# The heads stage of a GLA layer: DMA queues in the source's order, gates and states asked later, reciprocal roots on VectorE

## The chip, the cores and the metric

The kernel runs on one core of one Trainium2 chip. A core has five engines that work side by side, each with its own queue of instructions: TensorE (PE, matmul; PEld is its weight load), VectorE (DVE), ScalarE (ACT), GpSimd (POOL) and SyncE (SP, which here only issues DMAs). The metric is the time of one execution in device microseconds.

## The reference

One step of a two-layer streaming encoder, width D = 2048: 512 rows of a prompt, and 8 running streams of 16 rows each, 640 rows in all. Layer 0 is stick-breaking attention, layer 1 gated linear attention (GLA) with 4 heads, keys of 256 and values of 512. The change lies in layer 1. Cut to what matters:

```python
def gla_chunk(S, inp):                     # per chunk, S is the state (DK, DV) of a head
    q, k, v, g = inp                       # g = log a_t, the decay of each key dimension
    b = jnp.cumsum(g, axis=1); b_last = b[:, -1]
    q_in = q * jnp.exp(b)
    a = tril(einsum('bchd,bshd->bhcs', q_in, k * jnp.exp(-b)))
    o = einsum('bhcs,bshe->bche', a, v) + einsum('bchd,bhde->bche', q_in, S)
    S = exp(b_last)[..., None] * S + einsum('bshd,bshe->bhde', k * exp(b_last[:, None] - b), v)
    return S, o

q, k, v, r, a_lr = split(h @ w_in, ...)    # the plain products of layer 1
g = log_sigmoid(a_lr @ w_a2 + b_a) / 16
o = o * rsqrt(mean(o * o, axis=-1) + EPS) * g_out      # one norm per row and head
y = (o * silu(r)) @ w_out
```

## The kernel before, in words

Products in fp32 are done as three matmuls of a type that keeps fewer bits: `split` and `halves` make of each weight piece a high part on ScalarE (`wh`, L134, a cast) and the rest on VectorE (`wl`, L135, a subtraction). A raw piece `wr` is 128 x 1024 of float32, 0.52 MB, in two buffers that SP loads (L71).

The change concerns the heads stage of layer 1, L1508 to 1971. When it begins, the values `gv`, the gates `gr` and head 0's `gq` and `gk` are on their way to scratch tensors in DRAM. In the stage TensorE runs the rest of the layer's input product (`others`, `plain`, L632): the `q` and `k` columns of heads 1 to 3 in 24 weight pieces, 48 matmuls each on the two halves of the 640 rows (L654), two pieces to a result. A result leaves TensorE's bank by a ScalarE copy `pl` (L1519), and ScalarE stores it (L1521). The product has two banks. In the end stands the first part of the output product (`share`, L700) with its copies `y` (L708) and sums (L705).

Between the pieces of this product, side lanes put in their own work, each a Python generator:

- `decays`: loads `wa2`, `q`, `k` of a head, makes the decay (matmul L1647, Abs, Exp, Ln, scan, Exp: L1648 to 1673).
- `prompt_lane`: 16 units (4 heads x 4 chunks of 128 rows). `fetch` loads two tiles `v`, `fetch_gate` one tile `gate` (L71). A unit makes scores, output `o` and state `S`; `normed` (L1580) squares and sums on ScalarE (L1584) and asks `rstd_of` for the reciprocal root: mean plus EPS on VectorE (`on_ms`, L232), then a power of -0.5 on GpSimd (`on_r`, L234). `scaled_by` (L1588, ScalarE) applies it; `leave` (L1602) turns it, multiplies the gate in (L1607), and ScalarE stores it as `og` (L1610).
- `sample_lane`: the 8 streams, all at once for each head; their old states `s0` are loaded by GpSimd's DMAs (`move`, L78), eight buffers, and stored updated. `vst`, a stack of their values, is loaded by GpSimd too. One norm per head.
- `fetches`: loads `og` back and splits it for the output product.

`step(t)` in a lane and `side.after(t, f)` count in `pe["now"]`, a sum of estimated TensorE times that runs as the code is written out; they decide where in the written order a piece of work stands. TensorE's queue is the written order throughout. The queues of the other engines are put in order by a scheduler, which may move an instruction ahead of others of its engine. Both kernels give each DMA of SP and ScalarE the next of eight completion semaphores in turn; a DMA waits until the one that used its semaphore before has landed.

## Time and profile before

| what | value |
|---|---|
| median of 3 runs | 2514.42 us (2511.73 to 2514.44) |
| profiled execution | 2514.76 us, span 2513.0 us |
| granted clock of TensorE, mean | 0.984 |
| TensorE busy | 2427.7 us, 97% |
| VectorE, ScalarE, GpSimd busy | 63%, 40%, 5% |
| TensorE, share of the chain that ended last | 78% |

The profile is of one execution. The prediction shows rows of these views: busy time by windows; waits (engine, line and tile, released by which instruction: total, times, longest); timelines (start, duration, engine, line, operation, out<-in, shape, and in brackets the idle time before it with its releaser). Times in rows are us from the start of the span. The heads stage runs from about 1960 to 2400 us.

### The profile page before, as it was taken

The numbers are of one execution on the slowest core, as the hardware profiler recorded it, in microseconds if no ns is written. First come the engines' busy times: TensorE is split into PE (matmuls) and PEld (weight loads), VectorE is DVE, ScalarE is ACT, GpSimd is POOL, SyncE is SP. The second block draws the span as 40 slices with busy tenths as digits, with TensorE's granted clock in tenths as the row PEclk, the third lists the DMA queues.
The fourth block names the chain that finished last, engine by engine and source line by source line (L and its number), as shares of the span: only waits on it lengthen the run. The fifth ranks groups of instructions, "written<-read, shape, count | busy, mean of one in ns | idle before, by whom it ended". The sixth has DMA issues, their size and how long they took to land.

```text
span 2513.0 us, 43986 instructions
## 1 busy us (share of the span) xinstructions
PE 2427.7 (97%) x17561; PEld 2150.1 (86%) x17561; DVE 1580.6 (63%) x2566; ACT 994.1 (40%) x1731; POOL 135.2 (5%) x350
## 2 busy tenths in 40 slices
PE   6899999999999999999999999999999999999998
PEld 4589999899999998888887767999999989987776
DVE  5575555555666655666776568766676466675556
ACT  4332222222223334555544245333333455565223
POOL 0010000000000000000000000000000212332000
PEclk8899999999999999999999999999999999999999
DMA  9966666667664357777874664443534758976634
GB/s 343 330 210 216 224 205 208 221 214 226 209 202 126 110 166 227 256 243 236 259 235 146 187 226 134 129 118 110 145 104 117 209 183 271 294 265 218 226 114 147
DMA packets 487502, 503.12 MB, mean 200 GB/s; under 512 B 42746, under 2 KB 387202, under 8 KB 487170
## 3 DMA queue, kind: packets, MB, share of 16 engines
q1 hardware_dynamic: 456978, 441.85, 55.8%
q0 software_dynamic: 12848, 41.43, 4.8%
q10 hardware_dynamic: 17472, 17.04, 2.0%
q8 instruction: 138, 2.26, 0.4%
q14 instruction: 66, 0.54, 0.1%
HBM read 411.10 MB, written 89.13 MB: 199 GB/s over the span
## 4 chain that ended last, share of the span: by engine, by line
PE 78%; DMA 6%; DVE 4%; ACT 3%; issue 1%; SPq 0%; POOL 0%; ACTq 0%; POOLq 0%; DVEq 0%
PE ps_mm L595 40%; PE ps_mm L700 9%; PE ps_mm L654 9%; PE ps_mm L369 3%; PE ps_tp L1086 2%; DMA gv<-kr 2%; PE ps_tp L1559 2%; PE ps_mm L519 1%; PE ps_tp L1046 1%; PE ps_tp L1138 1%; PE ps_z L1022 1%; PE ps_z L180 1%; PE ps_mm L2042 1%; PE ps_z L1100 1%; PE ps_z L222 1%
## 5 line engine op out<-in xcount | busy, mean ns | idle before, releaser
L595 PE MATMUL ps_mm<-sums,wh 128*128 128x320 f32 x2752 | 613.5, 311 | 1.5 <-ACT wh L134 1.5
L595 PE MATMUL ps_mm<-h,wh 128*128 128x320 f32 x2064 | 462.8, 312 | 4.7 <-DVE u L601 4.7
L595 PEld LDWEIGHTS ps_mm<-sums,wh 128*128 128x128 f32 x2752 | 457.9, 188 | 10.4 <-issue 7.4
L595 PE MATMUL ps_mm<-sums,wl 128*128 128x320 f32 x1376 | 425.3, 309 | 0.7 <-DVE wl L135 0.7
L135 DVE TENSOR_TENSOR wl<-wr,wh 128x1024 fp32r<-128x1024 f32 x193 | 236.1, 1224 | 232.3 <-ACT wh L134 228.9
L595 PEld LDWEIGHTS ps_mm<-h,wh 128*128 128x128 f32 x2064 | 344.0, 188 | 20.7 <-issue 14.6
L134 ACT CAST wh<-wb 128x1024 fp32r<-128x1024 f32 x170 | 178.4, 1050 | 426.5 <-PE ps_mm L595 350.3
L134 ACT CAST wh<-wr 128x1024 fp32r<-128x1024 f32 x193 | 202.5, 1050 | 329.3 <-PE ps_mm L595 186.7
L595 PE MATMUL ps_mm<-h,wl 128*128 128x320 f32 x1032 | 319.3, 309 | 0.0
L654 PE MATMUL ps_mm<-h,wh 128*128 128x320 f32 x1152 | 265.7, 318 | 8.8 <-ACT pl L1519 6.3
L595 PEld LDWEIGHTS ps_mm<-sums,wl 128*128 128x128 f32 x1376 | 258.3, 188 | 1.0 <-DVE wl L135 1.0
L135 DVE TENSOR_TENSOR wl<-wb,wh 128x1024 fp32r<-128x1024 f32 x170 | 207.8, 1223 | 62.7 <-ACT wh L134 62.5
L654 PEld LDWEIGHTS ps_mm<-h,wh 128*128 128x128 f32 x1152 | 193.7, 190 | 23.5 <-issue 8.9
L700 PE MATMUL ps_mm<-wh,ogh 128*128 128x512 f32 x450 | 197.3, 438 | 7.2 <-ACT y L708 4.0
L595 PEld LDWEIGHTS ps_mm<-h,wl 128*128 128x128 f32 x1032 | 194.2, 188 | 0.0
L654 PE MATMUL ps_mm<-h,wl 128*128 128x320 f32 x576 | 178.8, 310 | 0.0
L700 PE MATMUL ps_mm<-wl,ogh 128*128 128x512 f32 x450 | 177.2, 394 | 0.3 <-DVE wl L135 0.3
L700 PE MATMUL ps_mm<-wh,ogl 128*128 128x512 f32 x450 | 177.2, 394 | 0.3 <-DVE ogl L135 0.3
L700 PEld LDWEIGHTS ps_mm<-wh,ogh 128*128 128x128 f32 x450 | 85.0, 189 | 35.7 <-issue 14.3
L654 PEld LDWEIGHTS ps_mm<-h,wl 128*128 128x128 f32 x576 | 109.1, 189 | 0.2 <-DVE wl L135 0.2
L700 PEld LDWEIGHTS ps_mm<-wh,ogl 128*128 128x128 f32 x450 | 84.7, 188 | 20.3 <-DVE ogl L135 0.7
L519 PE MATMUL ps_mm<-wh,h 128*128 128x512 f32 x252 | 93.2, 431 | 5.7 <-ACT h L134 3.7
(359 smaller groups left out, 3712.9 us busy)
## 6 DMA issues: line engine op xcount, KB each, us to landing
ar<-in_w_ada_dram SPq DMA_DIRECT2D x160, 512.0 KB
wb<-in_sb_w_in_dram SPq DMA_DIRECT2D x82, 512.0 KB
kc<-in_cache_sb_k_dram SPq DMA_DIRECT2D x64, 512.0 KB
vc<-in_cache_sb_v_dram SPq DMA_DIRECT2D x64, 512.0 KB
wr<-in_gla_w_in_dram SPq DMA_DIRECT2D x51, 512.0 KB
wb<-in_gla_w_in_dram SPq DMA_DIRECT2D x45, 512.0 KB
wr<-in_sb_w_in_dram SPq DMA_DIRECT2D x44, 512.0 KB
ar<-in_w_ada_dram SPq DMA_DIRECT2D x64, 256.0 KB
```

The source lines that it names most:

```text
L134: nc.scalar.copy(hi, x)
L135: (e or dve).tensor_tensor(lo, x, hi.bitcast(F32), op=ALU.subtract)
L180: mm(acc[32 * q:32 * q + 32, :w], cT[:, kt + m, :], by(cT[:, kt + m, :], rs[m // each][:, m % each, q, :]), start=kt + m == 0, stop=kt + m ...
L222: mm(acc[32 * j:32 * j + 32, :256], cT[:, kt + m, :], by(cT[:, kt + m, :], r[:, 256 * j:256 * j + 256]), start=kt + m == 0, stop=kt + m == ...
L369: mm(acc[a], l[:, c], by(l[:, c], r[:, k2, :]), start=kt == k0 and first, stop=kt == k0 + nk - 1 and last)
L519: mm(acc[a], l, by(l, r[:, e, :]), start=j == 0 and e == 0 and begun, stop=j == 7 and e == 1 and last)
L595: mm(acc, l[:, k, :], by(l[:, k, :], r), start=start and k == 0 and first, stop=k == 7 and last, skip_group_check=True)
L654: mm(acc[nt], l[:, k, :], by(l[:, k, :], r), start=k0 == 8 and k == 0 and first, stop=k0 == 0 and k == 7 and last)
L700: mm(acc, l, by(l, r[:, e, :]), start=i == 0 and e == 0 and first, stop=i == 1 and e == 1 and last)
L1022: mm(z[:, :n], q[:, hh, qs], by(q[:, hh, qs], k[:, hh, :n]), start=True, stop=True)
L1086: turn_block(tp[:, P * c:P * c + P], block(kc[:, c, P * hh:P * hh + P]), ident)
L1559: mm(out, l[a], by(l[a], r[b]), start=start and n == 0, stop=stop and n == 2, skip_group_check=True)
```

## The change

Three things, all in layer 1's heads stage.

1. For this stage SP's and GpSimd's queues too are in the written order, as TensorE's is. The scheduler still orders ScalarE's and VectorE's.
2. Places in the written order: the first two gates are asked at 40 and 44 us of estimated TensorE time instead of 14 and 16 (each later one 6 instead of 7 us after the store that frees its buffer), the eight first states from 26 on instead of from 18, the sample lane's first fetch at 30 instead of 12.
3. The 20 norms' reciprocal roots come from nine VectorE operations on 128 x 1 (`rstd_dve`: the mean, a first guess from the float's bits, one cubic and one quadratic refinement) instead of one on VectorE and one on GpSimd. Other norms of the kernel still use `rstd_of`.

```diff
+I32 = mybir.dt.int32
...
+    def rstd_dve(pool, ss, n, name):
+
+        ms, r, t, u = (pool.tile([P, 1], F32, tag=f"{name}_{x}", name=f"{name}_{x}", bufs=2 if x == "r" else 1) for x in ("ms", "r", "t", "u"))
+        dve.tensor_scalar(ms, ss, 1.0 / n, EPS, op0=ALU.mult, op1=ALU.add)
+        dve.tensor_scalar(r.bitcast(I32), ms.bitcast(I32), -0.5, float(0x5F3759DF), op0=ALU.mult, op1=ALU.add)
+        for cubic in (True, False):
+            dve.scalar_tensor_tensor(t, r, ms, r, op0=ALU.mult, op1=ALU.mult)
+            if cubic:
+                dve.tensor_scalar(u, t, 0.375, -1.25, op0=ALU.mult, op1=ALU.add)
+                dve.tensor_scalar(u, t, u, 1.875, op0=ALU.mult, op1=ALU.add)
+            else:
+                dve.tensor_scalar(u, t, -0.5, 1.5, op0=ALU.mult, op1=ALU.add)
+            dve.tensor_tensor(r, r, u, op=ALU.mult)
+        return r
...
             tc.tile_pool(name="w4", bufs=1, reuse_waits="tile") as w4:
+        loads = ExitStack()
+        loads.enter_context(tc.manual_schedule(engines={mybir.EngineType.SP, mybir.EngineType.Pool}))
...
-            return on, rstd_of(gl, s1, 512, "on"), o
+            return on, rstd_dve(gl, s1, 512, "on"), o
...
-                side.after(14.0 + 2.0 * u, lambda u=u: fetch_gate(u))
+                side.after(40.0 + 4.0 * u, lambda u=u: fetch_gate(u))
...
-                    side.after(7.0, lambda: fetch_gate(u + GP))
+                    side.after(6.0, lambda: fetch_gate(u + GP))
...
-            side.after(18.0 + 2.0 * n, ask)
+            side.after(26.0 + 2.0 * n, ask)
...
-            yield step(12.0)
+            yield step(30.0)
             here = fetch(0)
...
         side.finish()
+        loads.close()
```

The change adds lines, so that L1519 of before is L1537 after, L1588 is L1606, L708 is L724, L71 is L72. In the rows below, numbers behind names count tiles: `wr` is a raw weight piece, `gr_3` a store of layer 1's gate, `alr_in` the low-rank input of the decay.

SP's queue at the start of the stage, before (weight pieces 2 and 3 of the plain product are `wr_20615` and `wr_20677`):

```order
L71 DMA wr_20615<-in_gla_w_in_dram 128x8x128
L71 DMA wr_20677<-in_gla_w_in_dram 128x8x128
L74 DMA gr_3_106<-out_20288 128x640
L74 DMA gr_3_106<-out_20289 128x640
L71 DMA alr_in_20577<-alr_d_115 96x640
L71 DMA wa2_20593<-wa2_d_116 96x256
L71 DMA v_20595<-gv_0_0_107 128x512
L71 DMA v_20596<-gv_0_1_108 128x512
L71 DMA q_20665<-gq_0_95 128x1280
L71 DMA k_20666<-gk_0_99 128x1280
L71 DMA v_20693<-gv_0_0_107 128x512
L71 DMA v_20694<-gv_0_1_108 128x512
```

Then follow two more `v`, three gates, and weight pieces 4 and 5. SP's queue at the same place after (pieces 2 to 5 are `wr_20617`, `wr_20679`, `wr_20757`, `wr_20835`):

```order
L72 DMA alr_in_20579<-alr_d_115 96x640
L72 DMA wa2_20595<-wa2_d_116 96x256
L72 DMA v_20597<-gv_0_0_107 128x512
L72 DMA v_20598<-gv_0_1_108 128x512
L72 DMA wr_20617<-in_gla_w_in_dram 128x8x128
L72 DMA q_20667<-gq_0_95 128x1280
L72 DMA k_20668<-gk_0_99 128x1280
L72 DMA wr_20679<-in_gla_w_in_dram 128x8x128
L72 DMA v_20695<-gv_0_0_107 128x512
L72 DMA v_20696<-gv_0_1_108 128x512
L72 DMA wr_20757<-in_gla_w_in_dram 128x8x128
L72 DMA wr_20835<-in_gla_w_in_dram 128x8x128
```

The weight pieces 2 and 3 went from ahead of `gr` to behind the first `v` and behind `k`; pieces 4 and 5 went ahead of the gates, which now follow two more `v`.

ScalarE's queue at the store of the first `gq`, before:

```order
L1519 COPY pl_20679<-ps_mm_20553 128x320
L1648 ACTIVATE b_20697<-ps_tp_20715,cols_81 128x320
L1521 DMA gq_1_96<-pl_20679 128x640
L1651 ACT_TABLE_LOAD
L1651 ACTIVATE b_20697<-b_20697 128x640
L1652 ACT_TABLE_LOAD
```

And after:

```order
L1537 COPY pl_20681<-ps_mm_20555 128x320
L1666 ACTIVATE b_20699<-ps_tp_20717,cols_81 128x320
L1539 DMA gq_1_96<-pl_20681 128x640
L1669 ACT_TABLE_LOAD
L1669 ACTIVATE b_20699<-b_20699 128x640
L135 CAST wh_20753<-wr_20679 128x1024
L1670 ACT_TABLE_LOAD
```

The cast of weight piece 3, which stood ahead of this store, now stands in the middle of the decay's chain. In both the copy `pl` of the next result comes some ten rows further down.

GpSimd's queue, in words: before, eight states stood ahead of the six `vst` loads; after, three states, the six `vst` loads, five states. In between the 20 powers are gone.

ScalarE's queue at the last prompt unit, near a copy `y` of the output product, before:

```order
L1584 ACTIVATE on_24232,oss_24231<-ps_tp_24179 128x512
L1857 CAST kst0_20581<-ps_tp_24202 48x512
L1610 DMA og_3_94<-gate_24115 512x1x128
L1588 ACTIVATE on_24232<-ps_tp_24179,on_r_24236 128x512
L1766 ACTIVATE ps_tp_24249<-ps_tp_24249,ed_23482 128x512
L708 COPY y_24263<-ps_mm_24213 128x512
```

And after, where the same unit's scaling is L1606:

```order
L1602 ACTIVATE on_24398,oss_24397<-ps_tp_24343 128x512
L1875 CAST kst0_20583<-ps_tp_24366 48x512
L1628 DMA og_3_94<-gate_24261 512x1x128
L1784 ACTIVATE ps_tp_24422<-ps_tp_24422,ed_23610 128x512
L724 COPY y_24436<-ps_mm_24377 128x512
L135 CAST ogh_24499<-og_in_23686 128x640
L1606 ACTIVATE on_24398<-ps_tp_24343,on_r_24401 128x512
```

The scaling went from ahead of the copy `y` to behind it. VectorE's rows between this norm's sum and the end of its root, after:

```order
L241 TENSOR_SCALAR on_ms_24400<-oss_24397 128x1
L1625 TENSOR_TENSOR gate_24261<-ps_tp_24391,gate_24261 128x512
L242 TENSOR_SCALAR on_r_24401<-on_ms_24400 128x1
L1875 CAST kst1_20584<-ps_tp_24366 48x512
L244 SCALAR_TENSOR_TENSOR on_t_24402<-on_r_24401,on_ms_24400 128x1
L246 TENSOR_SCALAR on_u_24403<-on_t_24402 128x1
L247 TENSOR_SCALAR on_u_24403<-on_t_24402,on_u_24403 128x1
L1786 SCALAR_TENSOR_TENSOR S_23964<-S_23964,el_23609,ps_tp_24422 128x512
L250 TENSOR_TENSOR on_r_24401<-on_r_24401,on_u_24403 128x1
L244 SCALAR_TENSOR_TENSOR on_t_24402<-on_r_24401,on_ms_24400 128x1
L249 TENSOR_SCALAR on_u_24403<-on_t_24402 128x1
L250 TENSOR_TENSOR on_r_24401<-on_r_24401,on_u_24403 128x1
```

The eight added operations do not stand together: three larger ones, and of these one that needs ScalarE, lie between them.

## The prediction

> **What bounds the kernel now.** I read the page first, then busy time by stretches of the stage that the change touches (about 1960 to 2400 us), then TensorE's waits there, and then the timelines of the engines named in these waits. The page's first line on TensorE:

> ```profile
> PE 2427.7 (97%) x17561; PEld 2150.1 (86%) x17561; DVE 1580.6 (63%) x2566; ACT 994.1 (40%) x1731; POOL 135.2 (5%) x350
> ```

> TensorE is the bound, and the change leaves its instructions and their order as they are. So it can only move the time by TensorE's idle stretches and by its clock. Where these lie in the stage (columns: window, its length, then busy time of PE, PEld, DVE, ACT, POOL, then the granted clock, DMA share, GB/s):

> ```profile
> core 0: us, PE busy (x) PEld busy (x) DVE busy (x) ACT busy (x) POOL busy (x), PEclk, DMA share, GB/s
> 1980.00:2000.00 20.00, 20.00 (x138) 20.00 (x138) 6.28 (x10) 5.96 (x11) 7.38 (x16) 1.00 1.01 303
> 2000.00:2020.00 20.00, 13.73 (x84) 13.47 (x83) 10.32 (x19) 15.06 (x25) 0.00 (x0) 0.83 0.66 185
> 2020.00:2220.00 200.00, 199.95 (x1293) 181.56 (x1292) 124.02 (x227) 108.55 (x212) 52.13 (x92) 1.00 0.78 251
> 2260.00:2280.00 20.00, 18.07 (x85) 14.34 (x85) 13.15 (x25) 14.06 (x26) 6.01 (x12) 1.00 0.92 269
> 2320.00:2340.00 20.00, 18.07 (x86) 12.53 (x85) 13.45 (x19) 8.87 (x14) 7.11 (x13) 1.00 0.71 236
> 2340.00:2400.00 60.00, 57.37 (x248) 45.46 (x247) 25.66 (x32) 12.19 (x14) 0.00 (x0) 1.00 0.52 180
> ```

> One hole holds most of it: 6.27 us (20.00 - 13.73) in 2000 to 2020, with a lower clock behind it. Then come 1.93 us (C, at 2268), 1.93 us (D, at 2321) and 2.63 us in small pieces (E). From 2020 to 2220 there is nothing to gain. TensorE's waits in the stage (what waited, for whom: us in total, times, longest):

> ```profile
> PE ps_mm L654 <- ACT pl L1519: 6.3, 1, 6.3
> PE ps_mm L700 <- ACT y L708: 3.8, 2, 1.9
> PE ps_mm L369 <- DVE y L705: 1.5, 1, 1.5
> ```

> The first row is the hole (A). Its place on TensorE, and ScalarE's queue around it:

> ```profile
> 2008.07 0.31 PE L654 MATMUL ps_mm<-h,wl 128*128 128x320 f32 x1
> 2008.51 0.31 PE L654 MATMUL ps_mm<-h,wl 128*128 128x320 f32 x1
> 2015.08 0.90 PE L654 MATMUL ps_mm<-h,wh 128*128 128x320 f32 x2 [6.26 <-ACT pl L1519]
> ```

> ```profile
> 1994.14 1.05 ACT L134 CAST wh<-wr 128x1024 fp32r<-128x1024 f32 x1 [0.20 <-PE ps_mm L654]
> 1995.41 0.53 ACT L1648 ACTIVATE b<-ps_tp,cols 128x320 f32<-128x320 f32 x1
> 2002.59 0.33 ACTq L1521 DMA_DIRECT2D gq<-pl  x1
> 2002.95 1.28 ACT L1651 ACT_TABLE_LOAD   x1 [7.00 <-DMA v<-gv]
> 2005.00 1.28 ACT L1652 ACT_TABLE_LOAD   x1
> 2014.62 0.41 ACT L1519 COPY pl<-ps_mm 128x320 f32<-128x320 f32 x1
> ```

> ScalarE was free at 1995.9 and stood for 7.00 us at its own DMA issue, the store of `gq`, until a load of `v` had landed. The two have nothing to do with each other in the data: each DMA of SP and ACT takes the next of eight completion semaphores in the program, and waits until the one that used it before has landed. The chain of waits shows that load, issued 16.5 us before:

> ```profile
> 1986.01 16.50 DMA v<-gv
> ```

> Behind the store stand the decay's table loads, exponentials and casts, and only then the copy `pl` that frees TensorE's bank. That takes 11.7 us (2002.95 to 2014.62). Why the load was slow is seen in SP's queue and in the DMA queues from 1984 to 1992 (q1 carries SP's and ACT's transfers, q0 GpSimd's):

> ```profile
> 1977.83 0.37 SPq L71 DMA_DIRECT2D wr<-in_gla_w_in_dram  x1
> 1982.71 1.84 SPq L71 DMA_DIRECT2D v<-gv  x2
> 1985.28 0.68 SPq L71 DMA_DIRECT2D k<-gk  x1
> 1986.01 2.43 SPq L71 DMA_DIRECT2D v<-gv  x4
> 1990.07 10.30 SPq L71 DMA_DIRECT2D gate<-gr  x3
> 2000.93 4.83 SPq L71 DMA_DIRECT2D wr<-in_gla_w_in_dram  x2
> ```

> ```profile
> q0 software_dynamic: 504, 1.68, 56.5%
> q1 hardware_dynamic: 552, 1.25, 42.3%
> ```

> GpSimd's state and `vst` loads had more than half of the engines; SP's got 1.25 MB in 8 us, 0.156 MB per us, against 0.303 for all queues together.

> The lower clock behind the hole, and its absence behind C:

> ```profile
> 2015.00:2017.00 2.00, 1.92 (x7) 1.92 (x8) 0.71 (x3) 1.97 (x4) 0.00 (x0) 0.50 0.86 230
> 2017.00:2019.00 2.00, 2.00 (x12) 2.00 (x11) 1.89 (x3) 1.98 (x4) 0.00 (x0) 0.68 0.05 14
> 2270.00:2272.00 2.00, 1.05 (x5) 0.87 (x6) 1.12 (x3) 1.58 (x4) 0.90 (x2) 1.00 1.03 403
> ```

> At 0.50 and 0.68, two windows of 2 us lose 1.0 + 0.64 = 1.6 us of work. So A costs 6.3 + 1.6 = 7.9 us. The 1.93 us of C left the clock at 1.00. [...]

> **The change, part by part.**

> *SP's queue and the later gates: A.* In the new order SP issues, behind `gr`, `alr_in`, `wa2` and two `v`: weight piece 2, `q`, `k`, weight piece 3, two `v`, two weight pieces, two `v`, and only then the first gate. The store of `gq` now stands behind the fifth of these on its semaphore, the second `v`, issued before 1985. So the 7.00 us wait goes. What is late next is the weights: pieces 2 and 3 were issued by 1977.83, ahead of `gr`; now they are issued at about 1984.6 and 1986, behind it. Piece by piece, in the old clock of the trace:

> - TensorE's due times. Four matmuls in order take 0.147 us each (2008.07 to 2008.51 is three), a piece is 48 of them, 7.05 us, with some decay products between. Back from 2008.6, the end of piece 3, it needs piece 3 at about 2001 and piece 2 at about 1994.
> - Piece 2: the two `v` and the piece are 1.57 MB from 1982.7. At 0.156 MB/us they land at 1993, at 0.303 at 1988. I take 1992, since GpSimd's loads also start earlier. The cast takes 1.05 us and the subtraction 1.22 (below), so piece 2 is ready at 1994.4: stall 0.5, bounds 0 and 1.4.
> - Piece 3: `q`, `k` and the piece are 1.83 MB more: 6.0 to 11.7 us. I take 0.25 MB/us, since GpSimd's loads end early: 1999.3, ready at 2001.6, due at 2001.5. With its bounds 0 to 5.5; I take 0.6.
> - The copy `pl` for piece 4: ScalarE's new order has the cast of piece 3 ahead of the decay's second table load, so that chain starts at 1999.3 + 1.05 and takes, by the rows above, 9.6 us (2005.00 to 2014.62): 2010.0, and 0.41 for the copy, against 2008.6 + 1.1 by then: 0.7. Bounds 0 and 3.

> So A falls from 7.9 to about 1.8, a gain of 6.1, with bounds from 0.6 (the first rival) to 7.9. The clock stays up if no piece passes the 1.93 us that C had.

> *GpSimd's queue, states asked later.* Its eight states are no longer tied to TensorE's progress at the start: three go ahead of `vst`, five behind. The first loads may start some us earlier than before, which is in the rates above. The states' users come far later, in the stretch from 2020 with 199.95 of 200 us busy: nothing, from 0 to +2 (the largest single stall there would be like C's 1.93).

> *Reciprocal roots on VectorE.* Twenty norms lose one GpSimd power each and get eight more VectorE operations on 128 x 1, 160 in all. The nearest rows, the operation of this size, the subtraction that it can hold up, and ScalarE's wait for the powers:

> ```profile
> L232 DVE TENSOR_SCALAR on_ms<-oss 128x1 f32<-128x1 f32 x20 | 3.0, 150 | 10.1 <-ACT on L1584 9.9
> L135 DVE TENSOR_TENSOR wl<-wr,wh 128x1024 fp32r<-128x1024 f32 x43 | 52.6, 1223 | 29.3 <-ACT wh L134 28.9 <-DMA v<-gv 0.2
>   POOL on_r L234: 14.5, 9
> ```

> 160 x 0.150 = 24 us of VectorE over some 300 us in which it is 62% busy (124.02 of 200). Each norm's eight operations stand between others, so that what follows comes at most 8 x 0.150 = 1.2 us later. The cover is the lead of the weights and of the banks; where it is gone (C, D, E), a norm in each would cost up to 1.2 us. I take +0.5, bounds 0 and +4.

> *D.* ScalarE waited for GpSimd's power there, with the bank's copy behind it:

> ```profile
> 2317.78 0.15 DVE L232 TENSOR_SCALAR on_ms<-oss 128x1 f32<-128x1 f32 x1 [1.39 <-ACT on L1584]
> 2321.28 0.57 POOL L234 TENSOR_TENSOR on_r<-on_ms,mhalf 128x1 f32<-128x1 f32 x1
> 2321.88 0.69 ACT L1588 ACTIVATE on<-ps_tp,on_r 128x512 f32<-128x512 f32 x1 [2.97 <-POOL on_r L234]
> 2323.04 0.60 ACT L708 COPY y<-ps_mm 128x512 f32<-128x512 f32 x1
> ```

> GpSimd was held by its own state loads until 2321.28. In the new order the copy `y` stands ahead of the scaling, and the root comes from VectorE. VectorE's rows between `on_ms` and the root hold three larger operations of about 0.7 us and one that waits for ScalarE, so it comes 3 to 4 us after `on_ms`, hardly sooner than before: it is the copy's place that helps. I take -1.5 of the 1.93; bounds 0 and -1.93. C has the same copy behind a decay's chain and stays: 0, bounds -1.93 and +1.2. E's releaser is the addition on VectorE, in a tail that the change hardly touches: 0, bounds -1 and +1.

> **Sum.** -6.1 + 0 + 0.5 - 1.5 = -7.1 us. The profiled execution took 2514.76 us (span 2513.0 and 1.76 around it), 0.34 above the median shown, 2514.42. So 2507.7 on its own scale and 2507.3 on the median's: 2507.5.

> **The rivals.**

> 1. *The weights give it back.* If GpSimd's loads keep their share while pieces 2 and 3 are on the way, SP's rate stays at 0.156 MB/us. Then piece 2 is 1.4 us late; piece 3 lands at 2004.7, is ready at 2007, due at 2002.3: 4.7; the copy comes at 2015.4 for 2014: 1.2. That is 7.3 of the 7.9, and with D and the roots a gain of some 1.6: 2513. For it: 504 against 552 packets in the rows above, an even division for as long as both have work. [...] Against it: GpSimd's loads start earlier and should be done when pieces 2 and 3 need the engines. In this case the change does in effect not do what it says: it puts weights ahead of gates, but behind `gr`, `q` and `k`.
> 2. *The scaling on ScalarE waits longer, slower than before.* The nine operations of a root are spread over 8 to 22 rows of VectorE's queue, some of which wait for TensorE. In the last sample's norm, updates of states stand between them. ScalarE works in order, and its scaling waits for the root. Before, 14.5 us of such waits put 1.93 on TensorE, 13%. If waits come to 5 us at all 20 norms, 100 us, 13% is 13 us; with A's gain and without D's it is 2514.76 - 6.1 + 13 - 1.9 = 2519.8. It decides from about 8 us on TensorE, 60 us of waits, 3 us for each norm. Against it: the scaling's place in ScalarE's queue moves back as well.
> 3. *All of it.* SP's order feeds everything on time: A's 7.9, C's and D's 3.9, half of E's 2.6, less 0.5: -12.6, 2502. Against it: pieces 2 and 3 have no lead.

> **Chances.** About 0.2%, 5 us, is what a measurement of this kernel can tell from no change, so "faster" is below 2509.4. The forecast (2503 to 2510): 0.52. The first rival: 0.23. The second: 0.12. The third: 0.13. The forecast's range passes the bound by a little (0.03 of its chance), so faster 0.62, same 0.26, slower 0.12. The range takes in the first rival, and the third: 2501 to 2515. Outside remain the second and the ends.

> **What would show it.** Right: no wait of ScalarE at the store of `gq`, short waits of TensorE (below 2 us each) for `wl` near 1994 and 2001, a clock of 1.00 in the whole stage, no wait of 1.9 us for `y` at D, and VectorE some 24 us busier. Wrong: one wait above 3 us for `wl` or for the weights at piece 3 (first rival); waits for the root on ScalarE above 60 us in sum, with TensorE waiting for `y` or `pl` behind them (second); or waits of SP for a gate's buffer with a weight piece behind it that TensorE then waits for.

## The result, and the profile after

The changed kernel is slower: 2531.24 us median of 5 runs (2527.21 to 2535.07) against 2514.08 us of 5 runs before. The ratio is 1.0073, 95% interval 1.0059 to 1.0087. The profiled execution took 2531.24 us, span 2529.5 us. The forecast was 2507.5.

The page's line on TensorE after, to set beside that of before:

```profile
PE 2432.4 (96%) x17561; PEld 2150.2 (85%) x17561; DVE 1602.0 (63%) x2726; ACT 994.5 (39%) x1731; POOL 122.5 (5%) x330
```

The same instructions are there; VectorE is 21 us busier, GpSimd 13 us less. In the two profiles the stage's product begins at 1979.79 and at 1973.91 us. Ahead of the stage's own loads and memsets all queues hold the same instructions in the same order in both, and in the twelve experiments this start lies between 1974.4 and 1979.6: it varies by itself. So what follows compares the stage, from its first product (L654; L670 after) to the first product of the next one (L369; L385 after). The row of before, and below it the whole stage after and its three parts (window, length, busy PE, PEld, DVE, ACT, POOL, granted clock, DMA share, GB/s):

```profile
1979.79:2392.24 412.45, 399.36 (x2292) 342.73 (x2293) 245.89 (x422) 212.34 (x391) 98.67 (x178) 0.99 0.76 244
```

```profile
1973.91:2408.75 434.84, 408.94 (x2293) 345.98 (x2293) 267.56 (x582) 212.69 (x391) 82.50 (x152) 0.98 0.71 233
1973.91:2014.00 40.09, 37.04 (x249) 36.51 (x250) 18.88 (x31) 21.92 (x38) 4.81 (x10) 1.00 0.80 253
2014.00:2220.00 206.00, 199.83 (x1264) 178.97 (x1264) 134.74 (x321) 108.25 (x210) 43.68 (x80) 0.99 0.73 234
2220.00:2408.75 188.75, 172.07 (x784) 130.51 (x782) 113.95 (x232) 82.52 (x145) 34.02 (x62) 0.96 0.68 227
```

The stage takes 434.84 instead of 412.45 us: 22.4 more in these two profiles, 12.8 of it idle time of TensorE (25.9 against 13.1) and 9.6 longer busy time. At a clock of 0.50 TensorE was busy for 15.56 us after (from 2201.82, 2253.01, 2266.67 and 2338.35 on) and for 3.22 us before (from 2011.47 on); that is 6.2 us of lost speed. What made the other 3.4 us is not shown. The first 40 us are better than before: 3.05 us idle and a clock of 1.00. The middle, which had no idle time, now has 6.2 us, and the last part 16.7. TensorE's waits in the stage after, and ScalarE's longest (engine, line, tile, releaser: total, times, longest):

```profile
PE ps_mm L716 <- ACT y L724: 6.8, 3, 5.5
PE ps_tp L1665 <- DVE s L1902: 3.9, 1, 3.9
PE ps_z L1894 <- DMA s<-in_state_gla_dram: 2.8, 1, 2.8
PE ps_mm L670 <- ACT pl L1537: 2.7, 1, 2.7
PE ps_tp L1872 <- DVE kc L1867: 2.4, 1, 2.4
PE ps_tp L1900 <- DVE gate L1625: 1.6, 1, 1.6
```

```profile
ACT wh L135 <- DMA wr<-in_gla_w_in_dram: 28.0, 8, 7.0
ACT wh L135 <- DMA wr<-in_gla_w_out_dram: 22.5, 3, 10.7
```

These two are the heart of it. Before, no cast in the stage waits for a weight load (one stands 3.2 us, put down to a load of `x`); after, ScalarE stands for 50.5 us at eleven casts of weight pieces. The longest of these waits, 10.7 us near the stage's end, is no loss by itself: at the same cast before, ScalarE waited 10.4 us for TensorE. TensorE seldom waits for the weights themselves: once, 0.4 us for a `wl`. It waits for what stands behind the cast in ScalarE's queue, or in VectorE's behind the subtraction: copies of banks, `kc`, a gate. (The row of 2.8 us is a state that GpSimd loads.) The longest stall, in the chain that ended last, from a gate's store to TensorE's resumption (start, length, what):

```profile
2320.02 0.68 DVE gate L1625
...
2320.72 4.85 DMA og<-gate
...
2325.62 0.52 SPq L72
...
2326.23 7.66 DMA wr<-in_gla_w_out_dram
...
2333.91 1.05 ACT wh L135
...
2337.54 0.66 ACT ps_tp L1784
2338.20 0.52 ACT y L724
...
2338.77 1.65 PE ps_mm L716 x3
```

SP's and ScalarE's queues at the same place:

```profile
2310.50 15.64 SPq L72 DMA_DIRECT2D gate<-gr  x2
2326.23 1.15 SPq L72 DMA_DIRECT2D wr<-in_gla_w_out_dram  x2
```

```profile
2327.15 0.59 ACT L724 COPY y<-ps_mm 128x512 f32<-128x512 f32 x1
2333.91 1.04 ACT L135 CAST wh<-wr 128x1024 fp32r<-128x1024 f32 x1 [6.17 <-DMA wr<-in_gla_w_out_dram]
2337.54 0.66 ACT L1784 ACTIVATE ps_tp<-ps_tp,ed 128x512 f32<-128x512 f32 x1 [1.53 <-DVE on_r L242]
2338.12 0.59 ACT L724 COPY y<-ps_mm 128x512 f32<-128x512 f32 x1
```

SP stood until about 2325.6 at the second of two gates, whose buffer an `og` store still held. The two weight pieces behind it, which needed nothing from that store, went out at 2326.23 and landed 7.66 us later. ScalarE waited 6.17 us for the first, and the copy `y` that TensorE needed is the sixth instruction behind its cast.

The 3.9 us for `s` came by another way, at 2262.6. ScalarE's queue, and in the chain the store that it stood for:

```profile
2253.45 0.54 ACTq L1628 DMA_DIRECT2D og<-gate  x1
2254.03 0.53 ACT L1666 ACTIVATE b<-ps_tp,cols 128x320 f32<-128x320 f32 x1 [8.64 <-PE ps_z L1894]
```

```profile
2239.32 14.05 DMA og<-gate
```

ScalarE stood here at its own DMA issue, as it did at A before. In the traces before and after, the DMAs of SP and ScalarE signal on eight completion semaphores, 151 or 152 DMAs on each, and both `og` stores are on the same one: its last signal for the first is at 2253.37, 14.05 us after that store's issue, and the second went out at 2253.45. The view puts the wait down to TensorE, whose product for this `b` (L1665) had ended at 2245.40. The decay whose chain stands behind this store then came late for TensorE. By an estimate from these rows that cost 3.9 us of idle time and, with the clock at 0.50 from 2266.67 to 2273.50, 2.9 us of speed.

### The profile page after: what moved, and what is told of

It is laid out like the page before. It is cut to its first block, busy times and chain, and to the rows that moved or that the text cites. A ratio compares the mean times of both kernels' runs of the same rounds, so it can differ in the third digit from the quotient of the medians.

```text
span 2529.5 us, 44075 instructions
## 1 busy us (share of the span) xinstructions
PE 2432.4 (96%) x17561; PEld 2150.2 (85%) x17561; DVE 1602.0 (63%) x2726; ACT 994.5 (39%) x1731; POOL 122.5 (5%) x330
## 4 chain that ended last, share of the span: by engine, by line
PE 75%; DMA 7%; DVE 5%; ACT 4%; issue 2%; SPq 0%; ACTq 0%; POOL 0%; POOLq 0%; DVEq 0%
PE ps_mm L611 40%; PE ps_mm L716 9%; PE ps_mm L670 7%; PE ps_mm L385 3%; PE ps_tp L1102 2%; DMA gv<-kr 1%; PE ps_mm L535 1%; PE ps_tp L1577 1%; PE ps_tp L1062 1%; DMA wr<-in_gla_w_in_dram 1%; PE ps_tp L1154 1%; PE ps_z L181 1%; PE ps_z L1038 1%; DMA og<-gate 1%; ACT wh L135 1%
## 5 line engine op out<-in xcount | busy, mean ns | idle before, releaser
L611 PEld LDWEIGHTS ps_mm<-sums,wh 128*128 128x128 f32 x2752 | 458.0, 188 | 10.4 <-issue 7.4
L611 PEld LDWEIGHTS ps_mm<-h,wh 128*128 128x128 f32 x2064 | 343.0, 188 | 19.6 <-issue 11.7
L135 ACT CAST wh<-wb 128x1024 fp32r<-128x1024 f32 x170 | 178.3, 1049 | 425.3 <-PE ps_mm L611 356.7
L135 ACT CAST wh<-wr 128x1024 fp32r<-128x1024 f32 x193 | 202.5, 1050 | 356.0 <-PE ps_mm L611 179.8
L670 PE MATMUL ps_mm<-h,wh 128*128 128x320 f32 x1152 | 264.1, 316 | 5.1 <-ACT pl L1537 2.7
L136 DVE TENSOR_TENSOR wl<-wb,wh 128x1024 fp32r<-128x1024 f32 x170 | 207.9, 1223 | 61.4 <-ACT wh L135 61.2
L670 PEld LDWEIGHTS ps_mm<-h,wh 128*128 128x128 f32 x1152 | 192.6, 189 | 19.5 <-issue 8.1
L716 PE MATMUL ps_mm<-wh,ogh 128*128 128x512 f32 x450 | 199.1, 442 | 10.4 <-ACT y L724 6.8
L670 PE MATMUL ps_mm<-h,wl 128*128 128x320 f32 x576 | 178.2, 309 | 0.4 <-DVE wl L136 0.4
L716 PEld LDWEIGHTS ps_mm<-wh,ogh 128*128 128x128 f32 x450 | 86.0, 191 | 39.7 <-issue 14.5
L670 PEld LDWEIGHTS ps_mm<-h,wl 128*128 128x128 f32 x576 | 108.4, 188 | 0.6 <-DVE wl L136 0.6
## 6 DMA issues: line engine op xcount, KB each, us to landing
ar<-in_w_ada_dram SPq DMA_DIRECT2D x160, 512.0 KB
wb<-in_sb_w_in_dram SPq DMA_DIRECT2D x82, 512.0 KB
kc<-in_cache_sb_k_dram SPq DMA_DIRECT2D x64, 512.0 KB
vc<-in_cache_sb_v_dram SPq DMA_DIRECT2D x64, 512.0 KB
wr<-in_gla_w_in_dram SPq DMA_DIRECT2D x51, 512.0 KB
wb<-in_gla_w_in_dram SPq DMA_DIRECT2D x45, 512.0 KB
wr<-in_sb_w_in_dram SPq DMA_DIRECT2D x44, 512.0 KB
ar<-in_w_ada_dram SPq DMA_DIRECT2D x64, 256.0 KB
```

The costliest lines, as they stand in the source:

```text
L135: nc.scalar.copy(hi, x)
L136: (e or dve).tensor_tensor(lo, x, hi.bitcast(F32), op=ALU.subtract)
L611: mm(acc, l[:, k, :], by(l[:, k, :], r), start=start and k == 0 and first, stop=k == 7 and last, skip_group_check=True)
L670: mm(acc[nt], l[:, k, :], by(l[:, k, :], r), start=k0 == 8 and k == 0 and first, stop=k0 == 0 and k == 7 and last)
L716: mm(acc, l, by(l, r[:, e, :]), start=i == 0 and e == 0 and first, stop=i == 1 and e == 1 and last)
```

## The experiments

Each was timed beside runs of the kernel before on the same chip; ratios are to those, with 95% intervals. "Stage" is its length in the run's profile, as above (412.4 before, 434.8 after).

| run | what | ratio | stage, us |
|---|---|---|---|
| the change | all | 1.0073 (1.0059 to 1.0087) | 434.8 |
| e1 | without SP's written order | 0.9988 (0.9979 to 0.9998) | 411.5 |
| e2 | without GpSimd's written order | 1.0111 (1.0091 to 1.0131) | 441.8 |
| e3 | roots back on GpSimd | 1.0092 (1.0069 to 1.0116) | 432.0 |
| e4 | the old places | 1.0090 (1.0073 to 1.0107) | 436.6 |
| e5 | later gates 14 instead of 6 | 1.0096 (1.0080 to 1.0112) | 440.6 |
| e6 | weights one piece earlier | 1.0015 (1.0005 to 1.0025) | 421.4 |
| e7 | SP's written order alone | 1.0101 (1.0084 to 1.0118) | 442.1 |
| e8 | roots on VectorE alone | 1.0003 (0.9992 to 1.0014) | 414.4 |
| e9 | e6, and the next part's first weights early | 0.9982 (0.9973 to 0.9991) | 411.1 |
| e10 | GpSimd's written order alone | 0.9975 (0.9963 to 0.9988) | 410.7 |
| e11 | the later places alone | 1.0005 (0.9994 to 1.0016) | 415.9 |
| e12 | e1 without the roots | 0.9977 (0.9968 to 0.9987) | 410.7 |

**One part taken out: e1 to e4.** The theory was that SP's written order makes the weights late; the rivals were GpSimd's order, the roots and the places.

e1, SP's queue back to the scheduler:

```diff
-        loads.enter_context(tc.manual_schedule(engines={mybir.EngineType.SP, mybir.EngineType.Pool}))
+        loads.enter_context(tc.manual_schedule(engines={mybir.EngineType.Pool}))
```

> The changed kernel with SP's queue given back to the scheduler; GpSimd's queue stays in written order, the later places and VectorE's roots stay. Theory SP (weight pieces stand behind gates and v loads in SP's queue, ScalarE stands at their casts for 55 us instead of 5): about 2507 to 2514, ScalarE's wait for weight loads back below 10 us, no wait of TensorE for y above 2 us. Theory GpSimd (states late) or theory roots (VectorE's chains hold banks): 2526 to 2532 still.

2508.18 us against 2511.49 before. ScalarE waits for no weight load in the stage, and no wait of TensorE for `y` (on ScalarE) is left. The whole loss goes with SP's order, and so does ScalarE's long wait at an `og` store.

e2, GpSimd's queue back to the scheduler:

```diff
-        loads.enter_context(tc.manual_schedule(engines={mybir.EngineType.SP, mybir.EngineType.Pool}))
+        loads.enter_context(tc.manual_schedule(engines={mybir.EngineType.SP}))
```

> The changed kernel with GpSimd's queue given back to the scheduler; SP's stays in written order. Theory SP: 2522 to 2532, the 5.5 us wait for y near 2333 is still there, ScalarE's waits for weights above 40 us. Theory GpSimd: 2514 to 2520, and the stall at the state loads near 2248 (about 5 us with what follows) is what goes.

2540.75 us, above what either theory named: next to SP's, GpSimd's written order does not cost, it saves. The wait for a state near 2248 is gone here, and there are longer ones for `y`. ScalarE's wait at an `og` store is there too (10.6 us), as in e3 and e4 (9.4 us each).

e3, `rstd_of(gl, s1, 512, "on")` in `normed` again:

> The changed kernel with the 20 roots back as one power on GpSimd, whose queue is now in written order. Theory SP: 2525 to 2540, no better than the change. Theory roots: 2512 to 2520, as the 160 small VectorE operations are gone.

2534.31 us: the roots are not the cause.

e4, the four numbers of before:

> The changed kernel with the four places of before (gates at 14 and 16, later gates 7 after the store, states from 18, the sample lane's fetch at 12). Theory SP: 2525 to 2545, since the first gates go ahead of weight pieces again and the later ones stay where they block. Theory places (the later asking is what costs): 2512 to 2520.

2534.79 us: nor are the places.

**The mechanism within SP's order: e5 to e7.** e5 moves the gates:

```diff
-                    side.after(6.0, lambda: fetch_gate(u + GP))
+                    side.after(14.0, lambda: fetch_gate(u + GP))
```

> The changed kernel with each later gate asked 14 instead of 6 us of written time after the store that frees its buffer, so that fewer weight pieces stand behind a waiting gate in SP's queue. Theory gates (the gates' waits for the og stores, 109 us of SP, hold the weights): 2512 to 2520, ScalarE's waits for weights below 25 us. Theory whole queue (gates, v, q and k alike): 2521 to 2529, a part of the loss. Theory places: 2530 or more, since asking later still would cost more.

2537.77 us. SP's waits for the `og` stores fell (7 of them with 67 us in place of 14 with 109), yet ScalarE's waits for weights did not go:

```profile
ACT wh L135 <- DMA wr<-in_gla_w_in_dram: 25.5, 5, 7.0
ACT wh L135 <- DMA wr<-in_gla_w_out_dram: 16.9, 3, 10.1
```

The gates alone are not what holds the weights: the first theory missed in the time and in the waits, and the second in the time. The time lies in the range of the third (the places), but e4, with the old places, is as slow, so it does not speak for it. No long wait at an `og` store is left here, and the loss is as large; the late weights suffice for it. The gate at the last units still stood ahead of the same two weight pieces, and at other pieces a `v`, which waits for TensorE, or a `k`, which waits for a `gk` store, stood there instead (in the change SP stands 72.8 us in seven waits of a `v` for TensorE's products of L1577, and 9.7 us in one of a `k`).

e6 leaves the blocking loads where they are and moves the weights. In the stage's product and in the parts of the output product written in it, each piece is asked when the split of its buffer's last piece is written, one piece earlier than in the change. The core of the edit, in `plain`:

```diff
+                if early and nt == 0 and raw is not None:
+                    nxt, raw, more = wsplit(raw, 8), more, piece(n + 3)
-                if nt == 0 and raw is not None:
+                elif nt == 0 and raw is not None:
                     nxt, raw = second if n == 0 and second else (wsplit(raw, 8), piece(n + 2))
```

> The changed kernel with every weight piece of the stage asked one piece earlier in the written order (as soon as its buffer's last piece is split), all else as in the change. Theory lead (the written order asks weights one piece later than the buffers allow, and whatever SP waits for ahead of them makes them late): 2505 to 2516, ScalarE's waits for weights below 15 us, no wait for y above 3 us. Theory v, gates and states themselves are late: 2525 to 2532 still.

2516.47 us, just above the first theory's range: four fifths of the loss are gone with SP's written order still in force, and the wait at an `og` store is gone too. The two signs of that theory missed: the waits for weights come to 19.4 us, and a wait for `y` of 5.3 us is left. ScalarE's waits for the stage's own weights fell from 28.0 to 1.2 us. What was left:

```profile
ACT wh L135 <- DMA wr<-in_gla_w_out_dram: 18.2, 3, 10.5
ACT wh L135 <- DMA wr<-in_gla_w_in_dram: 1.2, 1, 1.2
```

The three stand at pieces of the output product (10.5 us of them again at the cast near the end); the longest wait of TensorE, 5.3 us for `y`, is at the first two pieces of its next part, which this edit did not move and which stand behind the last two gates.

e7, the kernel before with SP's queue alone in written order:

> The kernel before with SP's queue alone in written order, nothing else changed. Theory SP: 2525 to 2545, with ScalarE's waits for weights above 40 us. Theory that the loss comes only together with the new places or the roots: 2508 to 2518.

2539.65 us, 1.0101: SP's order alone costs at least as much as the whole change (the intervals just touch), and here too without a long wait at an `og` store.

**The parts alone, and the rest of the weights: e8 to e12.** e8, the kernel before with the roots on VectorE:

> The kernel before with the 20 roots on VectorE alone. Theory D (the power on a held GpSimd queue put 1.9 us on TensorE): 2508 to 2513, the wait near 2321 gone. Theory roots cost (160 small operations delay what stands behind them): 2515 to 2520.

2512.84 us against 2512.71: nothing that can be told. The stall at D is gone as expected, but another took its place at C, where the turn of a unit's output now waits 3.5 us for the scaling, and the scaling, at 2263.11, 0.98 us for its root:

```profile
PE ps_mm L670 <- ACT pl L1537: 5.4, 1, 5.4
PE ps_tp L1624 <- ACT on L1606: 4.3, 3, 3.5
```

e9, e6 with the two pieces moved that it had left:

```diff
             if todo:
                 raws.append(raw(*todo.pop(0)))
+            elif early is not None and len(early) < 2:
+                early.append(wraw(w_of(g + 1, 0, len(early)), 2, 512))
...
-            first = [wraw(w_of(g + 1, 0, i), 2, 512) for i in range(2)]
+            first = ahead_of[g]
```

> The kernel of the run e6 with the two first weight pieces of the next part of the output product asked early too (before, they stood behind the last two gates, and a 5.3 us wait of TensorE for y was left there). Theory lead: 2508 to 2513, this wait gone, ScalarE's waits for weights below 15 us. Theory that the last units' gates themselves are late: 2515 to 2518 still, with the wait at another copy.

2509.94 us against 2513.51, 0.9982: with every weight asked as early as its buffer allows, the changed kernel is faster than the one before. As a measure of the lead, the time from the end of the subtraction that frees a weight's buffer to the issue of the next load into it, over the stage's 41 loads in each trace: before 1.4 us on average, with 26 loads out within 0.1 us; in the change 8.0 us and 12 loads; in e9 2.4 us and 26 loads. ScalarE's waits for weights in the stage:

```profile
ACT wh L135 <- DMA wr<-in_gla_w_in_dram: 1.7, 1, 1.7
ACT wh L135 <- DMA wr<-in_gla_w_out_dram: 0.9, 1, 0.9
```

e10, the kernel before with GpSimd's queue alone in written order:

> The kernel before with GpSimd's queue alone in written order. If GpSimd's order is what makes the run e1 faster than before: 2507 to 2511. If it is the places: 2511 to 2514, and the stall for pl at the stage's start as long as before (about 6 us).

2508.40 us, 0.9975, the lowest ratio of all. GpSimd's queue at the stage's start, before and in e10:

```profile
1982.15 2.25 POOL L78 DMA_DIRECT2D s<-in_state_gla_dram  x4 [6.88 <-DVE h L135]
1984.48 1.64 POOL L78 DMA_DIRECT2D s<-in_state_gla_dram  x3
1987.62 2.18 POOL L78 DMA_DIRECT2D vst<-gv  x4 [1.05 <-issue]
```

```profile
1971.71 3.21 POOL L78 DMA_DIRECT2D vst<-gv  x6
1974.96 0.58 POOL L78 DMA_DIRECT2D s<-in_state_gla_dram  x1
1978.19 2.20 POOL L78 DMA_DIRECT2D s<-in_state_gla_dram  x4 [2.66 <-DVE h L135]
```

All six `vst` loads are out by 1974.9 and seven of the eight states asked by 1984.3, in a stage that starts 4.0 us earlier than before (1975.80). They still hold 37.4 to 67.5% of the DMA engines in each 4 us from 1976 to 1992, but 0.3% from 1992 to 1996, where before, at the same distance from the stage's start (1996 to 2000), GpSimd's loads held 58.0%. SP's loads then have the engines nearly for themselves. ScalarE's wait at the store of `gq` shrinks from 7.00 us, and TensorE's for `pl` from 6.26 to 3.25:

```profile
1997.28 1.28 ACT L1653 ACT_TABLE_LOAD   x1 [3.98 <-DMA v<-gv]
```

C and D are gone too, by the stalls' lengths more than half of the gain (3.9 us beside 3.0 at A); why these two go with GpSimd's order was not tried.

e11, the four later places alone:

> The kernel before with the four later places alone, all queues by the scheduler. If the places make the run e1 faster: 2507 to 2511, the stall for pl at the stage's start about 3 us instead of 6, as gates no longer stand between v and the weights. If not: 2511 to 2515.

2514.28 us, 1.0005: nothing that can be told; the stall for `pl` is 4.5 us, between the two that were named.

e12, e1 with the powers on GpSimd:

> The run e1 without VectorE's roots (GpSimd's queue in written order with the powers in it, the later places, SP's queue by the scheduler). If the roots cost nothing and gain nothing, as alone: 2506 to 2511. If the powers hold GpSimd's written queue, or are held by it: 2511 to 2518.

2508.70 us, 0.9977: as e10, so neither the roots nor the places add to GpSimd's order.

The parts alone give 1.0101, 0.9975, 1.0003 and 1.0005, and their sum of 0.84% stands beside the measured 0.73%, within the intervals.

## Why the prediction was wrong

**The step that failed** is the one that costed SP's queue at one place. The term for SP's order was worked out for weight pieces 2 and 3 at the stage's start and put at nothing for the 20 later pieces and those of the output product. Measured, SP's order costs 0.85% in the change (1.0073 beside 0.9988 of e1, some 21 us) and 1.01% alone (e7, some 25 us). "The cover is the lead of the weights and of the banks" was taken from the trace of before, where from 2020 to 2220 TensorE is busy 199.95 of 200 us. That busy stretch was the scheduler's doing: it had put the weight loads about as far ahead as the two buffers allow (a lag of 1.4 us on average). In the written order a piece is asked one piece later, and behind loads whose waits have nothing to do with it (8.0 us). e6 and e9 show that it is this lead: given back, the loss is gone. The row of 199.95 said that there was nothing to gain, and I read it as though there were nothing to lose. The prediction also asked only of the store of `gq` what stands ahead of it on its semaphore. The new order put an `og` store behind another, 8.6 us of ScalarE; since e5 and e7 lose as much without this, it is a second way and not the cause of the whole. How much of the change's loss goes by each of the two was not measured apart.

**The mechanism was named, without a price.** The last sentence on what would show the forecast wrong has "waits of SP for a gate's buffer with a weight piece behind it that TensorE then waits for". It got no rival, no price and no chance. The part that it missed is whose wait it is: the 50.5 us are ScalarE's, and TensorE's own wait for a weight is 0.4 us. ScalarE works in order and holds the bank copies behind the cast: the one at 2333.91 had waited 6.17 us, and `y`, the sixth instruction behind it, began at 2338.12.

**A.** The direction was right. The store of `gq` waits no more, as forecast (its copy `pl` ended at 1991.91, and it went out at 1991.94), and what is late next is piece 2:

```profile
1989.79 1.04 ACT L135 CAST wh<-wr 128x1024 fp32r<-128x1024 f32 x1 [6.99 <-DMA wr<-in_gla_w_in_dram]
```

The stall there is 2.68 us for `pl` behind this cast, the whole first 40 us lose 3.05 us at full clock, instead of 7.9. The gain is 4.8 where 6.1 was forecast, within its bounds, but in part by luck: three small stalls were forecast, and it was one, for a bank copy behind piece 2's cast. The mis-sized piece is the landing: with the start 5.9 us earlier, my 1992 is 1986.1, and it was 1989.8. The sum had the bytes wrong as well: two `v` of 256.0 KB and a piece of 512.0 KB are 1.05 MB, not 1.57, so the rate was lower still than I took. GpSimd's loads did start earlier (from 1971.01 on; before, one at 1974.68 and the rest from 1982.15 on), but were not done: they held 45.3% of the engines from 1976.83 to 1989.79 (587 packets beside 1858 of SP's and ScalarE's, so by packets the division was not even there), and piece 2 took 11.77 us from issue to landing. The sum also takes the 1.6 us of clock as saved. In these 40 us it was; later in the stage stalls of 2.37 and 2.76 us each brought the clock to 0.50.

**GpSimd's order** was put at nothing, 0 to +2. Alone it is worth -0.25%, some 6 us (e10). The prediction had the cause of A's part in its own rows (q0 with 56.5% of the engines while `v` was on its way), but used it only for the first rival, as a danger to the weights.

**The roots**: -1.5 at D and +0.5 elsewhere were forecast. Alone they measure +0.03% (-0.08 to +0.14), with D's stall gone and one of 3.5 us at C: the estimate of 1 us cannot be told from this. In the change D's place has the 5.5 us stall shown above, by another cause.

**The rivals.** The first (weights late at the start) asked the right question for two pieces out of many; its condition, that GpSimd's loads keep their share, came true for piece 2. The second, slower, was right in sign and wrong in its place: ScalarE's scalings waited 10.2 us for roots in all, less than the 14.5 before, not 60. The third did not come.

## What to carry to other kernels

Where a scheduler's order is replaced by the written one, price every load of that queue, not the ones at the edge that is being mended: for each, what stands directly ahead, what that waits for, and how many buffers ahead the scheduler had asked it. Ask of each store, too, which DMA stands ahead of it on its semaphore (7.00 us of ScalarE before, 8.64 after). A stretch without idle time proves that its lead is enough as it is now, and nothing about what is left when the lead shrinks. And follow a late load to the in-order engine that first touches it: here the price was paid by the bank copies behind a cast (5.5 us of TensorE at the longest). If the written order is wanted, write each load where its buffer comes free.

## What the hardware showed

```profile
1986.78:1990.19 3.41, 1.76 (x12) 1.49 (x11) 0.00 (x0) 0.40 (x1) 0.00 (x0) 1.00 1.08 401
1990.19:1993.60 3.41, 2.01 (x12) 1.75 (x13) 2.15 (x3) 3.39 (x6) 0.00 (x0) 1.00 1.07 379
2198.41:2201.82 3.41, 1.25 (x9) 1.25 (x10) 2.22 (x8) 3.08 (x8) 0.00 (x0) 1.00 0.42 122
2201.82:2205.23 3.41, 3.41 (x12) 2.85 (x11) 0.82 (x2) 0.72 (x2) 0.00 (x0) 0.50 0.00 0
```

Over this stage in the 14 traces, each step at full clock in which TensorE was idle for 1.90 us or more was followed by a step at 0.50 (2.66 before; 2.16, 2.75, 3.28 and 3.42 after), and none with 1.75 us or less was. Of four between, 1.78 and 1.81 lowered it and two of 1.86 did not, one of them C before. So about half a step of idle time is what these runs show in this stage; elsewhere in the trace before, steps with 1.66 and 1.64 us idle (1059.16 to 1062.57, 1519.96 to 1523.37) were followed by 0.50 too, and one with 1.80 (929.45 to 932.86) was not. As the grid lies differently in each run, a stall near that length may be free in one execution and cost half a step of speed, some 1.7 us, in the next; that is an estimate from the grid and was not tried on one kernel. A step need not be idle throughout for the clock to fall: the drop at 2201.82 came after a step with only 2.16 us idle (3.41 less 1.25). Nor are short stalls free of the clock's price: those of 2.37 us and of 2.76 us (2249.59 to 2252.35) were each followed by 3.41 us at 0.50.
